# Softmax heads of a hybrid encoder layer: the 640 keys of a query tile split into 384 and 256 columns

## The chip, the cores and the metric

The kernel runs on one core of one Trainium2 chip. The metric is device microseconds of one execution, the median of several. Engines are named as the profile names them: PE is the matrix engine (PEld its weight loads, which run beside the matmuls), DVE the vector engine, ACT the scalar engine with the activation functions, POOL the general engine, SP the engine whose queue issues nearly all DMAs. All data is float32; the matmuls read it as the four-byte type that the profile prints as f32 or fp32r, and precision is kept by splitting a number into a high and a low part.

## The reference

One encoder layer over 2048 positions of width 1024: an attention sub-layer with two groups of eight heads (head width 64), then a squared-ReLU MLP. The change touches the second group, the chunked softmax heads:

```python
CHUNK, LEFT_CHUNKS = 64, 8
BAND = (LEFT_CHUNKS + 1) * CHUNK          # 576
s = jnp.einsum('bnqhd,bnkhd->bnhqk', qc, k_band) * (d ** -0.5)
s = s + bias[None, None]                  # by clipped relative position
s = jnp.where(valid, s, NEG_INF)
p = jax.nn.softmax(s, axis=-1)
out = jnp.einsum('bnhqk,bnkhd->bnqhd', p, v_band)
```

Each chunk of 64 queries sees its own chunk and the eight before it. A tile of 128 queries (two chunks) therefore needs 640 keys, of which a bias of -1e30 masks the 64 that each half does not see.

## The kernel before

**Stages.** Norm and input projections come first, then the attention of both head groups with projections and output-projection rows of other blocks as filler, then the MLP, whose products are formed by a Strassen-like scheme. The sequence is reversed in memory, so "earlier" keys lie at higher columns.

**The attention loop.** Queries are taken in four blocks of 512 (`g`), and the work is a list of units: `SB` (stick-breaking heads) and `CA` (chunked softmax heads). The list is fixed: for the query blocks 2 and 3 together, then 1, then 0, all SB units of the eight heads and then all CA units. Each unit has four steps, one for each tile `qi` of 128 queries. Step *i* of the loop emits, in this order: the transposes (`wt`) of a unit two units back, the softmax or scan of the current tile (`soft1`), the split of the transposed weights into `wth` and `wtl` (`parts`), the exponentials (`soft2`), two value products into `acc`, then the scores of the *next* tile (`scores`), and then as many filler matmuls (`pf`, `po`) as a running credit allows. The credit counts matmuls and steps, not time. PE, DVE, ACT and POOL run in exactly the order in which the program emits; only the DMA issues of this stage on SP may be placed elsewhere by the scheduling layer.

**A CA unit.** There are 32 of them (8 heads, 4 query blocks). For query blocks 0 to 2 all four tiles have 640 keys; in block 3, at the end of the stored sequence, they have 512, 384, 256 and 128. Queries and keys are loaded with a high and a low part: the two parts of a key column lie on partitions 0 to 63 and 64 to 127, and the query tile comes twice, so that two matmuls (`l` = 0 and 1), each with its own weight load from `q`, add up to one score product.

One PSUM bank holds 512 float32 columns, and 640 do not fit in one. So `size` gives `n` = 640 and `hn` = 512: the first 512 columns are the tile `cz`, one bank for each `qi`; the remaining 128 columns of all four tiles are computed at once, when the scores of `qi` = 0 are emitted, into one bank `ct` (four slices of 128 columns).

**What DVE does with it.** `tail(qi)` adds the bias to the `ct` part and takes the running minimum (the kernel works with negated scores), which needs `ct` alone; `soft1(qi)` does the same with the `cz` part and starts from the minimum that `tail` left. In the order of DVE `tail(qi + 1)` stands right behind `soft1(qi)`. Both write one row of scores `s`, which a single ACT instruction of 640 columns turns into exponentials `e`.

**Banks.** `ct`, `cz`, `wt` and the SB scores `z` share four PSUM banks (tag `z`). A new tile takes a bank that has been released, and its first matmul waits for the last reader of the tile before it in that bank.

Of the kernel before, what the change touches and what calls it, by code (L numbers as in the profile page):

```python
# [9 lines left out]
F32 = mybir.dt.float32  # L10
# [8 lines left out]
P = 128  # L19
# [6 lines left out]
TB = 512  # L26
# [53 lines left out]
def encoder_kernel(ctx, tc, xT, c, g1, g2, w_in, w_rest, gqk, bias, w_o, w1, w2, w_ada, b_ada, out):  # L80
# [2 lines left out]
    pe = Ordered(tc, nc.tensor)  # L83
    osp = Ordered(tc, nc.sync)

    WIN = 640
    cpool = ctx.enter_context(tc.tile_pool(name="cpool", bufs=1))
    dram = ctx.enter_context(tc.tile_pool(name="dram", bufs=1, space=DRAM))
    rp = ctx.enter_context(tc.tile_pool(name="rp", bufs=2))
# [5 lines left out]
    pz = ctx.enter_context(tc.tile_pool(name="pz", bufs=4, space=PSUM))  # L95
# [5 lines left out]
    def scratch(name, shape, *counts):  # L101
        return {i: dram.tile(shape, F32, name=name + "_".join(map(str, i))) for i in product(*map(range, counts))}
# [8 lines left out]
    scr_wo = scratch("scr_wo", [P, 2, KT, P], KT)  # L111
    scr_b = scratch("scr_b", [P, WIN], NH)
    scr_h = dram.tile([P, KT, 2, TB], F32, name="scr_h")
# [19 lines left out]
    def column(tag):  # L133
        small[tag].append(small[tag].pop(0))
        return small[tag][-1]
# [103 lines left out]
    if True:  # L239
# [183 lines left out]
        def prepare_bias(h):  # L423
            b = stp.tile([P, WIN], F32, tag="bg", name=f"b{h}", bufs=2)
            sp.dma_start(b, bias[h])

            def rest():
                pool.memset(b[0:HD, WIN - HD :], NEG)
                pool.memset(b[HD:P, 0:HD], NEG)
                sp.dma_start(scr_b[h,], b)  # L430

            behind.add(4, rest)
# [245 lines left out]
    if True:  # L678
# [16 lines left out]
        def load_k(ca, h, tb, n, nm):  # L695
            k = (kp1 if ca else kp0).tile([P, n * TB], F32R, tag=f"k{ca}", name=f"k{ca}_{h}_{nm}")
            r = (h % 2) * HD
            for i in range(n):
                for l in range(2):
                    ldq.dma_start(  # L700
                        k[l * HD : (l + 1) * HD, i * TB : (i + 1) * TB].bitcast(F32),
                        scr_k[ca, tb + i, h // 2][l, r : r + HD],
                    )
            return k
# [42 lines left out]
        class Unit:  # L747


            def __init__(self, h, g, first, last):  # L750
                self.h, self.g, self.first, self.last = h, g, first, last
                self.nm = f"{self.ca}_{h}_{g}"
                self.ws = []
                self.wt = {}
# [30 lines left out]
        class SB(Unit):  # L785
# [27 lines left out]
            def scores(self, qi):  # L813
                nm = f"{self.nm}_{qi}"
                c0 = qi * P if self.diag else 0
                n = TB - c0
                self.z = z = pz.tile([P, TB], F32, tag="z", name=f"z{nm}")
                qs = slice(qi * P, (qi + 1) * P)
                pe.matmul(z[:, :n], self.q[:, 0, qs], self.k[:, c0:], start=True, stop=False)
                pe.matmul(z[:, :n], self.q[:, 1, qs], self.k[:, c0:], start=False, stop=True)  # L820
# [28 lines left out]
        class CA(Unit):  # L849
            ca = 1  # L850

            def __init__(self, h, g):
                super().__init__(h, g, True, True)
                self.weight = 0.9 * (1 if g < NTB - 1 else 0.75)
                self.nk = min(2 * TB, S - g * TB)
                order = [3] + [kb for kb in (4, 2, 1, 0, 5, 6, 7) if kb < self.nk // P]
                self.blocks = [(kb, max(0, kb - 4), min(4, kb + 1)) for kb in order]

            def load(self):
# [6 lines left out]
                self.k = load_k(1, h, g, nk // TB, f"{g}")  # L866
                self.bt = op.tile([P, WIN], F32, tag="bias", name=f"bias{h}_{g}", bufs=2)
                n = min(WIN, nk)
                sp.dma_start(self.bt[:, :n], scr_b[h,][:, :n])
# [7 lines left out]

            def size(self, qi):
                n = min(WIN, self.nk - qi * P)
                return n, min(n, TB)  # L880

            def scores(self, qi):
                nm = f"{self.nm}_{qi}"
                n, hn = self.size(qi)
                if qi == 0 and n > hn:
                    self.tails = pz.tile([P, TB], F32, tag="z", name=f"ct{nm}")
                    for i in range(STEPS):
                        t = self.tails[:, i * P : (i + 1) * P]
                        ks = slice(i * P + TB, i * P + WIN)
                        for l in range(2):  # L890
                            pe.matmul(t, self.q[:, l, i * P : (i + 1) * P], self.k[:, ks], start=l == 0, stop=l == 1)
                self.z = z = pz.tile([P, TB], F32, tag="z", name=f"cz{nm}")
                ks = slice(qi * P, qi * P + hn)
                for l in range(2):
                    pe.matmul(z[:, :hn], self.q[:, l, qi * P : (qi + 1) * P], self.k[:, ks], start=l == 0, stop=l == 1)

            def tail(self, qi):
                nm = f"{self.nm}_{qi}"
                n, hn = self.size(qi)
                s = zp.tile([P, WIN], F32, tag="p", name=f"s{nm}")  # L900
                m = 3e38
                if n > hn:
                    m = column("m0")
                    t = self.tails[:, qi * P : (qi + 1) * P]
                    dve.tensor_tensor_reduce(s[:, hn:n], t, self.bt[:, hn:n], -1.0, 3e38, ALU.add, ALU.min, m)
                self.sm[qi] = (s, m)

# [240 lines left out]
        STEPS = 4  # L1148
# [146 lines left out]
    if True:  # L1295
# [355 lines left out]
        def plain(mb, i):  # L1651

            f = len(steps)
            steps.extend(Second(mb, i, j) for j in range(NP))
            spread = lambda *ns: [f + n for n in ns]
            if i == 6:
                update(mb, 0, 1, spread(0, 1, 2, 8), spread(4, 5, 6, 12))
            if i == 5:
                update(mb, 1, 1, spread(1, 2, 3, 9), spread(6, 7, 8, 13))
                wide = []  # L1660

                def slot(nm):
                    if not wide:
                        t = raw_pair([P, HK, TB], F32, nm)
                        wide.extend(t[:, n, :] for n in range(HK))
                    return wide.pop(0)

                if mb:
                    update(mb, 0, 0, spread(11, 11, 11, 11), spread(16, 16, 17, 17), slot)
                    update(mb, 1, 0, spread(13, 13, 14, 14), spread(18, 18, 19, 19), kept)  # L1670
                else:
                    update(mb, 0, 0, spread(11, 12, 13, 14), spread(16, 17, 18, 19))
                    update(mb, 1, 0, spread(15, 16, 17, 21), spread(20, 21, 22, 25), None, True)
            return f
# [115 lines left out]
        def outer(i, plan):  # L1790

            f = len(steps)
            steps.extend(Outer(i, q, k) for q in range(7) for k in range(HP))
            for g in range(HP // 2):
                for pr, (begin, gap) in plan["load"].items():
                    at(begin + gap * g, lambda pr=pr, g=g: half(i, pr, g))
                for pr, (begin, gap) in plan["sum"].items():
                    at(begin + gap * g, lambda pr=pr, g=g: half_sum(i, pr, g))
            for q in range(7):
                at(f + HP * q - 12, steps[f + HP * q].load)  # L1800
            for pr, b in ((5, "22"), (6, "12"), (2, "11"), (4, "21")):
                s = steps[f + HP * OUTER.index(pr)]
                at(f + HP * OUTER.index(pr) + (1 if b == "22" else -5), lambda s=s, b=b: s.load_x(b))
            return f
# [47 lines left out]
        for mb in (1, 0):  # L1852
# [3 lines left out]
            for j in range(NP):  # L1856
                f = steps[begin + 7 * j]
# [32 lines left out]
        f = plain(0, 1)  # L1890
# [4 lines left out]
        for i, p in ((7, 6), (2, 5), (3, None), (4, None)):  # L1895
            f = outer(i, plan)
# [112 lines left out]
```

## Time and profile before

| | |
|---|---|
| median of 3 runs | 2556.95 us (2555.59 to 2557.69) |
| the profiled execution's own time | 2554.99 us |
| its span, first to last instruction | 2553.3 us |
| PE, share of the span | 99% |
| DVE, share of the span | 79% |
| ACT, share of the span | 59% |
| POOL, share of the span | 29% |
| DMA, mean over the span | 274 GB/s |

The three CA passes lie in the profiled execution at about 571 to 700 us (query blocks 2 and 3, sixteen units), 881 to 960 us (block 1, eight units) and 1204 to 1285 us (block 0, eight units).

How to read the rows: a group row gives line, engine, operation, output and inputs by the program's names, the shape and the count, then the time in which at least one of the group ran, the mean duration of one in ns, and the idle time of the engine before them. Matmuls overlap: one has a duration of 270 to 470 ns from its start to its modelled end, but the next starts much sooner. What a matmul costs PE is therefore the distance from its start to the next start, which the timeline gives: its rows begin with the start in us and the length in us of a run of like instructions. Most helper calls carry line 42, that of the wrapper that keeps the program order.

### The profile page before, as it was taken

The page shows a single profiled execution, that of the slowest core. Times are in us where ns is not written, and L with a number is a line of the kernel's source. Part 1 is how long each engine was busy: PE and PEld are TensorE (multiplying, and loading weights), DVE is VectorE, ACT ScalarE, POOL GpSimd, SP SyncE. Part 2 cuts the span into 40 slices and gives each one's busy share as a digit, 9 for nine tenths or more (in the row PEclk, how much of TensorE's full clock was granted, in tenths as well). Part 3 has the DMA queues.
Part 4 walks back from the last instruction along what each step waited for, and adds up shares of the span by engine and source line. Part 5 has one row for each costly group of instructions (what it writes and reads, how often), then busy time and mean ns, then how long its engine had stood idle before and what let it go on. Part 6 is the DMA issues. An engine that isn't in the chain of part 4 may idle for free. (4 is left out here: it accounts for less than half of the span.)

```text
span 2553.3 us, 39361 instructions
## 1 busy us (share of the span) xinstructions
PE 2528.9 (99%) x12436; PEld 2104.6 (82%) x12436; DVE 2010.0 (79%) x3509; ACT 1496.9 (59%) x2871; POOL 747.7 (29%) x1128
## 2 busy tenths in 40 slices
PE   9999999999999999999999999999999999999999
PEld 7888888888888888887888888888888888888887
DVE  7656767887789878998768777668988766988897
ACT  6333425668866677666755555566555555656565
POOL 4330144776776667776620000000000000000000
PEclk9999999999999999999999999999999999999999
DMA  9879979789977798756787888787899789777772
GB/s 362 324 296 364 343 275 296 214 240 289 277 233 234 242 270 276 254 188 208 213 301 258 301 277 289 252 313 262 277 317 312 262 274 396 273 282 270 286 264 83
DMA packets 293200, 698.92 MB, mean 274 GB/s; under 512 B 31360, under 2 KB 83584, under 8 KB 281856
## 3 DMA queue, kind: packets, MB, share of 16 engines
q1 hardware_dynamic: 291696, 691.69, 79.1%
q10 hardware_dynamic: 1296, 4.72, 0.5%
q8 instruction: 98, 1.61, 0.2%
q14 instruction: 110, 0.90, 0.1%
HBM read 477.66 MB, written 218.63 MB: 273 GB/s over the span
## 5 line engine op out<-in xcount | busy, mean ns | idle before, releaser
L42 PE MATMUL ps<-h,opw 128*128 128x512 f32 x1512 | 358.6, 389 | 0.0
L42 ACT CAST wth<-wt 128x512 fp32r<-128x512 f32 (+3 forms) x544 | 257.4, 484 | 172.5 <-PE wt L42 162.5
L42 POOL TENSOR_TENSOR b<-p 128x512 f32<-128x512 f32 (+1 forms) x320 | 292.5, 914 | 168.0 <-DVE p L42 91.5
L42 DVE TENSOR_TENSOR wtl<-wt,wth 128x512 fp32r<-128x512 f32 (+3 forms) x544 | 290.6, 546 | 59.4 <-ACT wth L42 57.1
L42 PEld LDWEIGHTS ps<-h,opw 128*128 128x128 f32 x1512 | 283.7, 188 | 58.9
L42 PE MATMUL pt<-w,ht 128*128 128x512 f32 x1248 | 288.2, 391 | 0.0
L42 PE MATMUL ps_s<-h,opw 128*128 128x512 f32 x1152 | 277.3, 390 | 0.3 <-ACT cp L42 0.3
L42 PEld LDWEIGHTS pt<-w,ht 128*128 128x128 f32 x1248 | 233.0, 188 | 47.7
L42 DVE TENSOR_TENSOR_SCAN p<-z,p,zero 128x512 f32<-128x512 f32 x192 | 245.6, 1280 | 25.8 <-ACT z L42 18.6
L42 PE MATMUL ps<-oph,opv 128*128 128x512 f32 x1152 | 263.2, 390 | 0.7 <-ACT opv L42 0.6
L42 PEld LDWEIGHTS ps<-oph,opv 128*128 128x128 f32 x1152 | 215.9, 188 | 47.3 <-ACT opv L42 1.5
L42 PEld LDWEIGHTS ps_s<-h,opw 128*128 128x128 f32 x1152 | 215.9, 188 | 46.0 <-ACT cp L42 0.8
L42 PE MATMUL acc<-wth,v 128*128 128x512 f32 (+3 forms) x544 | 220.7, 410 | 0.0
L42 ACT CAST opr<-r 128x512 fp32r<-128x512 f32 x224 | 139.4, 623 | 105.9 <-PE ps L42 50.1
L42 ACT ACTIVATE z<-z 128x512 f32<-128x512 f32 (+1 forms) x320 | 166.5, 521 | 55.3 <-PE z L42 49.5
L42 PE MATMUL z<-k,q 128*128 128x512 f32 (+3 forms) x640 | 185.6, 371 | 7.7 <-DVE p L42 7.0
L42 PE MATMUL acc<-wtl,v 128*128 128x512 f32 (+3 forms) x544 | 185.5, 347 | 0.0
L42 PE MATMUL ps<-opr,ol 128*128 128x512 f32 x768 | 176.4, 389 | 0.1
L42 PE MATMUL wt<-ident,b 128*128 128x128 f32 x1088 | 171.4, 273 | 0.9 <-DVE cols L42 0.3
L42 DVE TENSOR_TENSOR opr<-r,opr 128x512 fp32r<-128x512 f32 x224 | 150.7, 686 | 25.9 <-ACT opr L42 23.3
L42 PEld LDWEIGHTS wt<-ident,b 128*128 128x128 f32 x1088 | 136.4, 141 | 42.1 <-DVE cols L42 1.8
L42 PEld LDWEIGHTS ps<-opr,ol 128*128 128x128 f32 x768 | 144.0, 188 | 30.5 <-DVE ol L42 0.4
(214 smaller groups left out, 4845.6 us busy)
## 6 DMA issues: line engine op xcount, KB each, us to landing
q<-scr_q SPq DMA_DIRECT2D x128, 256.0 KB, 5.0
w<-in_w_dram SPq DMA_DIRECT2D x64, 512.0 KB, 5.7
r<-scr_hid SPq DMA_DIRECT2D x64, 512.0 KB, 7.7
k<-scr_k SPq DMA_DIRECT2D x240, 128.0 KB, 4.5
v<-scr_v SPq DMA_DIRECT2D x120, 256.0 KB, 4.4
wa<-in_w_ada_dram SPq DMA_DIRECT2D x48, 512.0 KB, 6.2
ow<-scr_wo SPq DMA_DIRECT2D x24, 1024.0 KB, 6.5
hw<-scr_hid SPq DMA_DIRECT2D x48, 512.0 KB, 6.6
```

Source lines behind the costliest of these rows:

```text
L42: return lambda *x, **y: self.tc.keep_in_program_order(f(*x, **y))
```

## The change

The bank of the first part is cut at `NEAR` = 384 columns instead of 512, and so the remaining part has 256 columns instead of 128. Four remaining parts of 256 columns need two banks; the first (`qi` 0 and 1) is computed with the scores of `qi` = 0, the second (`qi` 2 and 3) with those of `qi` = 1. The CA units of query block 3 keep their single part.

```diff
-    WIN = 640
+    WIN, NEAR = 640, 384
...
+                self.tails = {}
...
             def size(self, qi):
                 n = min(WIN, self.nk - qi * P)
-                return n, min(n, TB)
+                return n, NEAR if n > TB else n
...
-                if qi == 0 and n > hn:
-                    self.tails = pz.tile([P, TB], F32, tag="z", name=f"ct{nm}")
-                    for i in range(STEPS):
-                        t = self.tails[:, i * P : (i + 1) * P]
-                        ks = slice(i * P + TB, i * P + WIN)
+                if qi < 2 and n > hn:
+                    ct = pz.tile([P, 2, WIN - NEAR], F32, tag="z", name=f"ct{nm}")
+                    for i in (2 * qi, 2 * qi + 1):
+                        self.tails[i] = t = ct[:, i % 2, :]
+                        ks = slice(i * P + NEAR, i * P + WIN)
                         for l in range(2):
                             pe.matmul(t, self.q[:, l, i * P : (i + 1) * P], self.k[:, ks], start=l == 0, stop=l == 1)
...
-                    t = self.tails[:, qi * P : (qi + 1) * P]
+                    t = self.tails.pop(qi)
```

**Where it moves PE's work.** The scores of the first tile of the unit of head 4, query block 0 (names end in the head, the query block and the tile; the last number is a buffer's). Before, behind the value products of the unit before it:

```order
L42 MATMUL acc_1_0_15856<-wth_1_0_0_15878,v_1_0_15557 128x128
L42 MATMUL acc_1_0_15856<-wtl_1_0_0_15879,v_1_0_15557 128x128
L42 MATMUL ct_4_0_0_15925<-k_4_0_15624,q_4_0_15621 128x128 x8
L42 MATMUL cz_4_0_0_15934<-k_4_0_15624,q_4_0_15621 128x512 x2
L42 MATMUL po_1_15702<-fx_5_15299,ow_1_15061 128x512
L42 MATMUL po_1_15702<-fx_6_15301,ow_1_15061 128x512
```

Now:

```order
L42 MATMUL acc_1_0_15876<-wth_1_0_0_15898,v_1_0_15575 128x128
L42 MATMUL acc_1_0_15876<-wtl_1_0_0_15899,v_1_0_15575 128x128
L42 MATMUL ct_4_0_0_15945<-k_4_0_15638,q_4_0_15635 128x256 x4
L42 MATMUL cz_4_0_0_15950<-k_4_0_15638,q_4_0_15635 128x384 x2
L42 MATMUL po_1_15721<-fx_5_15315,ow_1_15077 128x512
L42 MATMUL po_1_15721<-fx_6_15317,ow_1_15077 128x512
```

Four of the eight matmuls of the remaining part are gone from this place, and the others are twice as wide. The other four stand now ahead of the scores of the second tile, as PE's rows one step later show:

```order
L42 MATMUL acc_1_0_15876<-wth_1_0_6_15930,v_1_0_15575 128x256
L42 MATMUL acc_1_0_15876<-wtl_1_0_6_15931,v_1_0_15575 128x256
L42 MATMUL ct_4_0_1_15996<-k_4_0_15638,q_4_0_15635 128x256 x4
L42 MATMUL cz_4_0_1_16001<-k_4_0_15638,q_4_0_15635 128x384 x2
L42 MATMUL po_1_15721<-fx_6_15317,ow_1_15077 128x512 x2
L42 MATMUL po_1_15721<-fx_7_15319,ow_1_15077 128x512
```

Before, the `cz` pair of the second tile followed the `acc` products directly. Everything behind it stands where it stood.

**On DVE** nothing changes its place; the rows of the same unit now (before, the widths were 128, 512 and 128 in the rows of `s`, and the third of these rows read the same `ct` as the first):

```order
L42 TENSOR_TENSOR wtl_1_0_7_15935<-wt_1_0_7_15925,wth_1_0_7_15934 128x128
L42 ISA s_4_0_0_15975,cols<-ct_4_0_0_15945,bias_0_15643 128x256
L42 ISA cols 128x1
L42 ISA s_4_0_0_15975,cols<-cz_4_0_0_15950,bias_0_15643,cols 128x384
L42 ISA cols 128x1
L42 ISA s_4_0_1_15978,cols<-ct_4_0_0_15945,bias_0_15643 128x256
L42 ISA cols 128x1
```

The second `ct` of a unit takes the bank that the first tile's `cz` leaves, and so its first matmul waits for `soft1(0)`, as the second tile's `cz` did before. That `cz` now takes the bank of the first `ct`, and waits for its last reader `tail(1)`, one DVE instruction later. No other wait between the computing engines is new inside a CA unit. On SP the DMAs are the same, but some loads of the attention stage are issued a few places earlier or later.

## The prediction

> **What bounds the kernel now.** I read the page first, then the busy time of each engine in the three CA passes (the view by stretches), because the change acts in these alone.
>
> ```profile
> span 2553.3 us, 39361 instructions
> PE 2528.9 (99%) x12436; PEld 2104.6 (82%) x12436; DVE 2010.0 (79%) x3509; ACT 1496.9 (59%) x2871; POOL 747.7 (29%) x1128
> ...
> core 0: us, PE busy (x) PEld busy (x) DVE busy (x) ACT busy (x) POOL busy (x), PEclk, DMA share, GB/s
> 571.00:700.00 129.00, 125.87 (x767) 107.81 (x767) 95.25 (x356) 106.70 (x266) 91.65 (x91) 1.00 0.94 288
> 881.00:960.00 79.00, 78.43 (x479) 67.09 (x477) 61.98 (x220) 61.67 (x140) 51.26 (x43) 1.00 0.89 275
> 1204.00:1285.00 81.00, 80.03 (x494) 69.09 (x493) 64.52 (x223) 59.86 (x136) 54.03 (x50) 1.00 0.73 214
> ```
>
> PE is the bound: it idles 0.57 us of 79 in the second pass and 0.97 of 81 in the third, and the clock is 1.00 in each. DVE is at 78% and 80% there, ACT at 78% and 74%. The first pass differs: PE idles 3.13 us of 129, ACT is at 83% and the DMA engines at 0.94. So what PE saves in the last two passes should come out at the end almost whole; in the first it may partly turn into waiting.
>
> Busy time does not price a matmul, since matmuls overlap. The price is the distance from start to start, which PE's timeline over one CA unit of the third pass gives:
>
> ```profile
> 1264.70 0.27 PE L42 MATMUL acc<-wtl,v 128*128 128x128 f32 x1
> 1264.81 1.06 PE L42 MATMUL ct<-k,q 128*128 128x128 f32 x8
> 1265.71 0.68 PE L42 MATMUL cz<-k,q 128*128 128x512 f32 x2
> 1266.23 0.85 PE L42 MATMUL po<-fx,ow 128*128 128x512 f32 x3
> ...
> 1268.14 0.28 PE L42 MATMUL acc<-wth,v 128*128 128x256 f32 x1
> 1268.25 0.28 PE L42 MATMUL acc<-wtl,v 128*128 128x256 f32 x1
> 1268.37 0.63 PE L42 MATMUL cz<-k,q 128*128 128x512 f32 x2
> 1268.84 0.62 PE L42 MATMUL po<-fx,ow 128*128 128x512 f32 x2
> ...
> 1272.61 0.34 PE L42 MATMUL acc<-wth,v 128*128 128x384 f32 x1
> 1272.78 0.34 PE L42 MATMUL acc<-wtl,v 128*128 128x384 f32 x1
> 1272.96 0.63 PE L42 MATMUL cz<-k,q 128*128 128x512 f32 x2
> ```
>
> Eight `ct` matmuls of 128 columns take 1265.71 - 1264.81 = 0.90 us, 0.112 each. Two of 512 take 0.47 (1268.37 to 1268.84), 0.235 each. The rows of `acc` give 0.115 for 256 columns and 0.175 for 384. From 256 to 512 the price rises by 0.06 for 128 columns, and on that line 128 columns would cost 0.055. They cost twice that: 128 columns are as dear as 256. And the `cz` pair behind the eight takes 0.52 (1265.71 to 1266.23), 0.05 more than the pair at 1268.37, so the last narrow matmul also delays its successor. I read this as a floor of about 0.11 us below which a matmul with a weight load of its own does not go.
>
> **This is the whole case.** Columns (640) and matmuls (four) per tile stay the same, so under any price that is a straight line in the columns the change saves nothing. It saves only what lies between floor and line.
>
> **The cost on PE.** Only the 24 units with 640 keys change. A second source is each group's busy time divided by its runs of like matmuls, less the mean length, over the others' count:
>
> ```profile
> L42 PE MATMUL cz<-k,q 128*128 128x512 f32 x208 | 67.3, 404 | 0.4 <-DVE cols L42 0.4
> L42 PE MATMUL ct<-k,q 128*128 128x128 f32 x192 | 24.8, 272 | 0.7 <-DVE p L42 0.7
> L42 PE MATMUL cz<-k,q 128*128 128x384 f32 x16 | 4.1, 339 | 0.0
> L42 PE MATMUL cz<-k,q 128*128 128x256 f32 x16 | 3.3, 288 | 0.4 <-DVE cols L42 0.4
> ```
>
> For 256 columns: 3.3 / 8 pairs - 0.288 = 0.124; for 384: 4.1 / 8 - 0.339 = 0.174; for 512: 67.3 / 104 - 0.404 = 0.243; for `ct`: (24.8 / 24 - 0.272) / 7 = 0.109. These hold a few waits and are rounded to 0.1 us, the timeline's to 0.01. I take 0.118 for 256 (between 0.115 and 0.124) and 0.175 for 384. In one unit then:
>
> - `qi` 0: before 0.90 + 0.52 = 1.42. Now 4 x 0.118 + 2 x 0.175 + 0.05 (the first still stands behind a 128-wide `acc`) = 0.87. Saved 0.55.
> - `qi` 1: before 0.47. Now 4 x 0.118 + 2 x 0.175 = 0.82. Added 0.35.
> - `qi` 2 and 3: 0.35 for 0.47 each. Saved 0.24.
>
> The sum is 0.44 saved per unit, 24 x 0.44 = 10.6 us. With 0.124 and 0.174 it is 0.525 - 0.374 + 0.244 = 0.395, or 9.5 us; with the line's floor gone altogether it would be 0. I carry 0.42 as the middle: 10 us.
>
> The Trainium skill ("TensorE: Matmul & The Clock Gate", Back-to-back issue gap) gives about 81 ns for a sustained 128-column matmul and 131 for 512: a straight line through these makes the change worth nothing, and the rows above differ (112 and 235). The same page (LDWEIGHTS) gives 128 weight columns / 1.2 = 107 ns for a load; with the greater of that and N / 2.4 + 2.5 as an estimate, a unit saves 8 x (107 + 216 - 109 - 163) = 408 ns, 9.8 us in all, which this case's rows support.
>
> **The cost on DVE, ACT, POOL and SP.** DVE's instructions keep their count and order; only widths change.
>
> ```profile
> L42 DVE CUSTOM_DVE_ANT_0 s<-cz,bias,cols 128x512 f32<-128x512 f32 x32 | 23.9, 746 | 1.7 <-PE cz L42 1.5
> L42 DVE CUSTOM_DVE_ANT_0 s<-ct,bias 128x128 f32<-128x128 f32 x32 | 9.2, 287 | 3.9 <-PE ct L42 3.2 <-POOL p L42 0.7
> L42 DVE CUSTOM_DVE_ANT_0 s<-cz,bias 128x512 f32<-128x512 f32 x8 | 5.4, 680 | 0.0
> L42 DVE CUSTOM_DVE_ANT_0 s<-cz,bias 128x384 f32<-128x384 f32 x8 | 4.4, 547 | 0.0
> L42 DVE CUSTOM_DVE_ANT_0 s<-cz,bias 128x256 f32<-128x256 f32 x8 | 3.3, 415 | 0.0
> ```
>
> `tail` goes from 287 to 415 ns, `soft1` from 746 to 547 + (746 - 680) = 613: 1028 for 1033 per tile, nothing. ACT, POOL and the DMAs keep theirs. What changes is that PE leaves them 0.42 us less per unit of about 9.8 (the `ct` at 1264.81 and the next unit's at 1274.63), so DVE rises from 80% to about 83%, below PE.
>
> **The new wait.** The second tile's `cz` now waits for `tail(1)` instead of `soft1(0)`, and PE's queue stands behind it: its filler, the transposes of the next step, and through them ACT and DVE. The margin, from the timeline of all engines in the same unit:
>
> ```profile
> 1266.09 0.28 DVE L42 CUSTOM_DVE_ANT_0 s<-ct,bias 128x128 f32<-128x128 f32 x1
> 1266.53 0.75 DVE L42 CUSTOM_DVE_ANT_0 s<-cz,bias,cols 128x512 f32<-128x512 f32 x1
> 1267.20 0.08 DVE L42 DVE_READ_ACCUMULATOR2_ANT cols<- 128x1 f32 x1
> 1267.20 0.29 DVE L42 CUSTOM_DVE_ANT_0 s<-ct,bias 128x128 f32<-128x128 f32 x1
> 1267.41 0.08 DVE L42 DVE_READ_ACCUMULATOR2_ANT cols<- 128x1 f32 x1
> ```
>
> `soft1(0)` is through at 1267.28 and `cz` starts at 1268.37: 1.09 us to spare. Now PE gets there 0.55 sooner, at 1267.82, for the second `ct`; `tail(0)` is 0.13 longer and `soft1(0)` 0.13 shorter, so it is again through at about 1267.3, 0.5 to spare. `tail(1)`, 0.13 longer, ends at about 1267.65 with its read, while PE wants the bank at 1267.82 + 0.47 = 1268.29: 0.6 to spare. I cost it at nothing; DVE's being ahead covers it. If that cover went, every us by which DVE is late would be paid in each of 24 units.
>
> **Where the saving can get stuck.** In the first pass the short units of query block 3 have little filler. Two stalls from its timeline (after the arrow what ended the wait):
>
> ```profile
> 599.33 0.63 PE L42 MATMUL wt<-ident,e 128*128 128x128 f32 x4 [1.03 <-DVE cols L42]
> ...
> 618.09 0.44 PE L42 MATMUL cz<-k,q 128*128 128x128 f32 x2 [1.05 <-DVE cols L42]
> ```
>
> And of the pass's waits (us in total, times, longest) the largest of DVE and of PE:
>
> ```profile
> DVE wtl L42 <- ACT wth L42: 19.3, 37, 1.6
> ...
> PE cz L42 <- DVE cols L42: 1.6, 3, 1.1
> ...
> PE wt L42 <- DVE cols L42: 1.3, 2, 1.0
> ```
>
> PE's end on DVE, which itself waits in this pass for ACT. If PE arrives earlier and the others do not, such a wait grows by what PE saved. Eight of the 24 units lie here (3.4 us of the 10). Bounds: all of it lost, or none; I take 1.2 us lost, nearer to none, since 2.9 us of waits in two kinds are five occurrences for sixteen units. Result: a gain of 8.8 us.
>
> **The rivals.**
>
> 1. *The first pass keeps its length, and the others lose some.* ACT at 83% and DMA at 0.94 speak for it; against it stands that PE is idle there for 2.4% of the time only. Losing all 3.4 us of the first pass and a third of the 6.7 of the others leaves 4.5: 2552.5 us.
> 2. *A straight line prices the matmuls,* as the first of the page's figures would have it, or the floor comes from something else than width. Then the time stays at 2557. The eight `ct` at 0.112 beside 0.115 for 256 columns speak against it.
> 3. *Slower: the second tile's `cz` waits for `tail(1)`.* The two margins of 0.5 and 0.6 us are those of one undisturbed unit; in units where DVE runs later, PE would stop here. It must lose 10 / 24 = 0.42 us per unit to eat the gain, that is DVE must be a whole us later than in the rows above, in all units. At 0.7 per unit the result is 24 x 0.7 - 10 = 6.8 us slower, 2564. DVE at 80% speaks against it.
> 4. *That the change doesn't do what it says* (fewer narrow matmuls) is excluded by the order shown above.
>
> **How the numbers follow.** The sum stands against the profiled execution: 2554.99 - 8.8 = 2546.2. The median of the runs, 2556.95, lies 1.96 above that execution, so for the median I say 2548.1. A measurement of this kernel can tell about 0.2% (5.1 us) from no change. Forecast, a gain of 5.1 to 11.4 us: 0.84. Rival 1: 0.07, of which 0.01 would still count as faster. Rival 2: 0.03. Rival 3: 0.06. So faster 0.85, same 0.09, slower 0.06. The range reaches from a gain of 11.4 (11.0, the highest sum of the rows with 0.115, plus the runs' spread) to one of 4.0: 2545.5 to 2553.0, which leaves out about 0.13 above and 0.04 below.
>
> **What would show it.** `ct` must appear as 192 matmuls of 128x256 with about 0.118 from start to start, `cz` with 208 of 128x384 and 16 of 128x512. From the first `ct` to the filler behind it, a unit's 1.42 us must become about 0.87. The second and third pass must be about 3.4 us shorter each, the first by 2 or more, and the rest of the span unchanged. DVE's group for `ct` must read about 415 ns, for `cz` about 613. Wrong I would be if PE's waits for DVE before `ct` and `cz` (under 2 us now) grew to several us, if the passes kept their length while PE's idle time rose, or if 256-wide `ct` matmuls stood 0.15 us or more apart, since eight of them a unit then cost 0.26 more and most of the gain is gone.

## The result and the profile after

| | before | after |
|---|---|---|
| median of 11 runs each | 2557.03 us (2555.59 to 2558.37) | 2550.11 us (2548.36 to 2553.2) |
| ratio, 95% interval | | 0.9973 [0.9964, 0.9983] |
| the profiled execution's own time | 2554.99 us | 2549.72 us |
| its span | 2553.3 us | 2548.0 us |

The change gains 6.9 us; the interval reaches from 4.3 to 9.2. The forecast was a gain of 8.8 and a time of 2548.1. One execution of the kernel before, of 6549.87 us, is left out of all comparisons below.

The page of the changed kernel, span and busy time of the engines:

```profile
span 2548.0 us, 39355 instructions
PE 2520.9 (99%) x12436; PEld 2104.0 (83%) x12436; DVE 2010.0 (79%) x3509; ACT 1498.6 (59%) x2871; POOL 747.0 (29%) x1128
```

PE has 12436 matmuls as before and is busy 8.0 us less; DVE's busy time is the same to the tenth of a microsecond. The groups that changed, on PE and on DVE (busy us, mean ns of one, idle time before them):

```profile
L42 PE MATMUL cz<-k,q 128*128 128x384 f32 x208 | 54.3, 342 | 0.5 <-DVE cols L42 0.4
L42 PE MATMUL ct<-k,q 128*128 128x256 f32 x192 | 31.6, 287 | 1.7 <-DVE cols L42 1.0 <-DVE p L42 0.7
L42 DVE CUSTOM_DVE_ANT_0 s<-cz,bias,cols 128x384 f32<-128x384 f32 x96 | 58.7, 611 | 3.9 <-PE wt L42 0.5
L42 DVE CUSTOM_DVE_ANT_0 s<-ct,bias 128x256 f32<-128x256 f32 x96 | 40.3, 419 | 1.5 <-PE ct L42 1.2 <-issue 0.3
```

The counts are the 192 and 208 that the order showed. `tail` takes 419 ns and `soft1` 611, forecast 415 and 613. New is 1.0 us of waiting for `cols`, a result of DVE, ahead of `ct`: before, `ct` waited for DVE's `p` alone (0.7 us), which it still does.

**The price of the matmuls.** PE's timeline over one unit of the third pass: the second `ct`, then the `cz` of tiles 1, 2 and 3, then the next unit's first `ct` and `cz` (start, length, count of the run):

```profile
1261.89 0.64 PE L42 MATMUL ct<-k,q 128*128 128x256 f32 x4
1262.37 0.52 PE L42 MATMUL cz<-k,q 128*128 128x384 f32 x2
1262.72 0.62 PE L42 MATMUL po<-fx,ow 128*128 128x512 f32 x2
...
1264.41 0.52 PE L42 MATMUL cz<-k,q 128*128 128x384 f32 x2
1264.77 0.86 PE L42 MATMUL po<-fx,ow 128*128 128x512 f32 x3
...
1266.72 0.52 PE L42 MATMUL cz<-k,q 128*128 128x384 f32 x2
1267.08 0.62 PE L42 MATMUL po<-fx,ow 128*128 128x512 f32 x2
...
1268.28 0.69 PE L42 MATMUL ct<-k,q 128*128 128x256 f32 x4
1268.81 0.51 PE L42 MATMUL cz<-k,q 128*128 128x384 f32 x2
1269.15 0.40 PE L42 MATMUL po<-fx,ow 128*128 128x512 f32 x1
1269.83 1.06 PE L42 MATMUL wt<-ident,e 128*128 128x128 f32 x8 [0.28 <-DVE wtl L42]
```

From start to start the first tile takes 1269.15 - 1268.28 = 0.87 us, the second 1262.72 - 1261.89 = 0.83, the third and fourth 0.36 each: 2.42 us a unit. Before it was 1.42 + 3 x 0.47 = 2.83. So 0.41 is saved per unit, 9.8 us in 24 units. (The last row, a wait, comes up again below.)

**Where it comes out.** The three passes in stretches that begin at a pass's first `ct` and end at the same matmul in both kernels, 25 matmuls behind the pass's last `cz`. Columns: stretch, its length, busy time of PE, PEld, DVE, ACT, POOL with their instructions, granted clock, DMA share, GB/s. Before:

```profile
571.30:702.40 131.10, 127.97 (x782) 109.84 (x781) 95.64 (x356) 108.84 (x269) 92.32 (x92) 1.00 0.92 283
881.80:962.20 80.40, 79.83 (x488) 68.40 (x487) 62.04 (x221) 63.32 (x144) 52.73 (x44) 1.00 0.90 279
1205.00:1286.70 81.70, 81.45 (x505) 70.74 (x506) 64.36 (x226) 60.56 (x139) 55.19 (x49) 1.00 0.72 210
```

After:

```profile
571.50:699.50 128.00, 124.96 (x783) 109.65 (x781) 95.32 (x356) 108.78 (x269) 92.21 (x92) 1.00 0.94 290
878.90:957.70 78.80, 77.54 (x489) 68.43 (x489) 61.53 (x221) 63.26 (x144) 52.48 (x44) 1.00 0.87 258
1200.70:1280.40 79.70, 78.75 (x505) 70.72 (x505) 63.88 (x225) 60.50 (x139) 54.91 (x49) 1.00 0.73 215
```

With 0.41 a unit, each pass should be 3.3 us shorter. By the starts in the traces (to 0.01 us) the first is shorter by 3.17, the second by 1.65, the third by 1.98: 6.80 in all. In the first pass PE's idle time stays (131.10 - 127.97 = 3.13, then 3.04); in the second it grows from 0.57 to 1.26 and in the third from 0.25 to 0.95. So 3.0 of the 9.8 us are lost, nearly all in the second and third pass.

**The longest wait** is one in the second pass. PE's timeline of that unit before (after the arrow what ended a wait):

```profile
900.12 1.00 PE L42 MATMUL ct<-k,q 128*128 128x128 f32 x8
900.96 0.68 PE L42 MATMUL cz<-k,q 128*128 128x512 f32 x2
901.48 1.03 PE L42 MATMUL wt<-ident,e 128*128 128x128 f32 x8
...
903.05 0.40 PE L42 MATMUL acc<-wtl,v 128*128 128x512 f32 x1
903.68 0.50 PE L42 MATMUL cz<-k,q 128*128 128x512 f32 x1 [0.23 <-DVE cols L42]
```

The same unit after, all engines:

```profile
896.71 0.65 PE L42 MATMUL ct<-k,q 128*128 128x256 f32 x4
...
897.19 0.51 PE L42 MATMUL cz<-k,q 128*128 128x384 f32 x2
...
898.42 0.69 DVE L42 TENSOR_TENSOR stf<-pf,stf 128x512 fp32r<-128x512 f32 x1 [0.60 <-ACT stf L42]
...
899.03 0.41 DVE L42 CUSTOM_DVE_ANT_0 s<-ct,bias 128x256 f32<-128x256 f32 x1
899.12 0.40 PE L42 MATMUL acc<-wtl,v 128*128 128x512 f32 x1
...
899.59 0.62 DVE L42 CUSTOM_DVE_ANT_0 s<-cz,bias,cols 128x384 f32<-128x384 f32 x1
900.13 0.08 DVE L42 DVE_READ_ACCUMULATOR2_ANT cols<- 128x1 f32 x1
...
900.27 0.74 PE L42 MATMUL ct<-k,q 128*128 128x256 f32 x4 [0.76 <-DVE cols L42]
```

From the unit's first `ct` to the second tile's first score matmul it is 903.68 - 900.12 = 3.56 us before and 900.27 - 896.71 = 3.56 after. Between them runs a chain over DVE: it waits for ACT's half of a filler product's split (`stf`), does its own half in 0.69 us, and only then the softmax of the first tile, which releases the bank. PE's own work in between shrank by 0.5 us, the chain did not, so PE waits longer by what it saved: the `ct` comes 900.27 - 899.12 = 1.15 us behind the last `acc`, where 0.23 is normal behind 512 columns (899.12 - 898.88 for the `acc` before it was 0.24), so 0.92 are lost here. Before it was 903.68 - 903.05 = 0.63 behind the last `acc`, that is 0.40 lost: the wait grew by 0.52, nearly all that the first tile had saved. At the entry of the third pass the same is seen; before:

```profile
1204.99 1.11 PE L42 MATMUL ct<-k,q 128*128 128x128 f32 x8 [0.73 <-DVE p L42]
1205.94 0.68 PE L42 MATMUL cz<-k,q 128*128 128x512 f32 x2
1206.76 0.44 PE L42 MATMUL wt<-ident,b 128*128 128x128 f32 x2
```

After:

```profile
1200.70 0.74 PE L42 MATMUL ct<-k,q 128*128 128x256 f32 x4 [0.72 <-DVE p L42]
1201.28 0.62 PE L42 MATMUL cz<-k,q 128*128 128x384 f32 x2
1202.47 0.55 PE L42 MATMUL wt<-ident,b 128*128 128x128 f32 x3 [0.57 <-DVE p L42]
```

From `ct` to `wt` it is 1.77 us in both: the scan `p` of the SB unit ahead sets that moment, and the `ct` and `cz` done faster only end in a longer wait for it. The third pass loses nearly as much again in its last unit, where a transpose waits for DVE's `wtl` (the last row of the unit shown above): it starts 1269.83 - 1269.15 = 0.68 us behind the filler, where it was 1276.27 - 1276.04 = 0.23 in the kernel before, so 0.45 are lost.

The rest of the attention stage keeps its length but for small differences (the stretches between the passes 179.40 and 179.45, 242.78 and 243.02 us; from the third pass to the first `pso`, which ends the stage, 34.55 and 35.07). That `pso` starts at 1321.22 before and at 1315.47 after; the part behind it takes 1232.06 and 1232.53. These differences outside the passes add up to some 1.5 us, and so the two profiled executions differ by 5.3 us and not by 6.8; the change's second profile (below) shows that they scatter.

### The profile page after: what moved, and what is told of

Read it like the earlier page. It is cut to its first block, busy times and chain, and to the rows that moved or that the text cites. A ratio compares the mean times of both kernels' runs of the same rounds, so it can differ in the third digit from the quotient of the medians.

```text
span 2548.0 us, 39355 instructions
## 1 busy us (share of the span) xinstructions
PE 2520.9 (99%) x12436; PEld 2104.0 (83%) x12436; DVE 2010.0 (79%) x3509; ACT 1498.6 (59%) x2871; POOL 747.0 (29%) x1128
## 4 chain that ended last, share of the span: by engine, by line
PE 83%; DVE 6%; DMA 3%; ACT 3%; issue 2%; POOL 1%; SPq 0%; DVEq 0%; ACTq 0%; POOLq 0%
PE ps L42 27%; PE ps_s L42 14%; PE pt L42 11%; PE acc L42 6%; PE wt L42 6%; PE pf L42 4%; PE z L42 4%; PE po L42 4%; PE pq L42 3%; DVE p L42 2%; PE cz L42 2%; DMA hw<-in_w_dram 1%; PE ct L42 1%; DVE opr L42 1%; ACT z L42 1%
```

## The experiments

The theory F is that of the prediction: a floor of about 0.11 us per matmul with its own weight load, and so a saving only where narrow matmuls are replaced. N is a rival by which matmuls under 256 columns run at a lower rate rather than at a floor, P that the new place of the matmuls, not their width, brings the gain. Theory W, formed from the traces, says that what is missing to the sum went into the waits for DVE shown above.

### The cut at 448 columns: floor or rate

```diff
-    WIN, NEAR = 640, 384
+    WIN, NEAR = 640, 448
```

> The cut at 448 + 192 columns, everything else as in the change (two tiles of two remaining parts). Theory F (a floor: a matmul with its own weight load takes about 0.112 us however narrow, and from 256 columns up the price is a line through 0.118 and 0.235): 192 columns cost the floor, 0.112, and 448 cost 0.205, so PE saves 8 x 0.03 = 0.24 us per unit, 5.8 in all, of which some 2.5 to 3 are lost in waits as in the change: about 2554, between the two kernels, `ct` 0.112 apart. Rival N (narrow matmuls, under 256 columns, run at half rate: 0.112 is 128 columns at twice the price): 192 columns cost 0.168 to 0.177, PE loses 8 x 0.03 per unit instead: about 2563, slower than before, `ct` 0.17 apart. A straight line: 2557.

2552.63 us, ratio 0.9985 [0.9976, 0.9994]: 5.2 us faster than before. PE's timeline of a unit's second tile:

```profile
1263.25 0.59 PE L42 MATMUL ct<-k,q 128*128 128x192 f32 x4
1263.67 0.59 PE L42 MATMUL cz<-k,q 128*128 128x448 f32 x2
1264.10 0.62 PE L42 MATMUL po<-fx,ow 128*128 128x512 f32 x2
```

Four of 192 columns take 0.42 us, 0.105 each in this unit (the median distance over the whole trace is 0.112), no more than 128 columns did (0.112); two of 448 take 0.43. 192 columns still lie on the floor, and the gain is that of the narrower `cz` pairs. N falls, and so does the straight line of rival 2: 448 + 192 are the same 640 columns.

The kernel before has still narrower matmuls, eight of a single column at the start of the program:

```profile
12.49 1.05 PE L42 MATMUL pva<-ones,nsaa 128*128 128x1 f32 x8 [0.63 <-DVE nsaa L42]
13.40 2.25 PE L42 MATMUL idle<-ones 128*128 128x128 f32 x18
```

One column costs (13.40 - 12.49) / 8 = 0.114 us, as much as 128: the floor does not depend on the columns. What sets it stays open. Every matmul here has a weight load of its own (PE and PEld both count 12436), so no run separates the load from another fixed cost of a matmul.

### Two tiles for the remaining part, cut as before: structure alone

```diff
-    WIN, NEAR = 640, 384
+    WIN, NEAR = 640, 512
```

> The structure of the change alone: the cut stays at 512 + 128, but the four remaining parts stand in two tiles of two, computed with the scores of the first and second query tile. Theory F (the gain comes from the widths, and the two tiles bring only waits): PE's work is that of before plus 0.05 us per unit (a second run of narrow matmuls delays its successor), and PE reaches the second tile 0.45 us sooner, where it waits for DVE: 2558 to 2560, slower than before by 1 to 3 us. Rival P (the gain comes from where the second half of the remaining parts was put, not from the widths): 2550, as the change.

2556.35 us, ratio 0.9998 [0.9989, 1.0007]: no difference. Four of the eight 128-column matmuls stand here ahead of the second tile's scores, as in the change, and no gain shows: P falls. The slowdown that I had expected of F here did not come either; the new order of bank releases costs nothing measurable while PE's work keeps its length.

### The disputed price, doubled

The remaining part's products are formed twice; in the kernel before,

```diff
-                        for l in range(2):
+                        for l in (0, 1, 0, 1):
```

and the same edit in the changed kernel. Each adds 192 matmuls, here of 128 and there of 256 columns.

> The kernel before, with the eight matmuls of the remaining parts (128 columns) issued twice into the same bank. F and N: 8 x 24 more at 0.112 us each, 21.5 us, less up to 1 us of waits that they cover: 2577 to 2579. A straight line through the prices of 256 and 512 columns (0.055 for 128): 10.6 us, 2568.

> The change, with the matmuls of the remaining parts (256 columns) issued twice into the same bank. Theory F: 8 x 24 more at 0.118 us, 22.7, less 1 to 2.7 us of waits that they cover: 2570 to 2573, so as much over the change as the doubled 128-column matmuls cost over before (20.3), for twice the columns. A straight line in the columns: twice that, 2590.

The 128-column kernel takes 2576.95 us, ratio to before 1.008 [1.0064, 1.0096], 19.1 more than the 2557.83 of its session. The 256-column one takes 2569.49, ratio 1.0046 [1.0032, 1.006], 19.4 more than the change's 2550.11. With four runs each these are good to about 4 us; in the traces the three passes are longer by 19.8 and by 19.0 us. Twice the columns, the same addition. PE's timeline with 16 of 128 columns:

```profile
1262.44 1.95 PE L42 MATMUL ct<-k,q 128*128 128x128 f32 x16
1264.22 0.68 PE L42 MATMUL cz<-k,q 128*128 128x512 f32 x2
```

And with 8 of 256:

```profile
1269.47 1.12 PE L42 MATMUL ct<-k,q 128*128 128x256 f32 x8
1270.43 0.52 PE L42 MATMUL cz<-k,q 128*128 128x384 f32 x2
```

These are 1.78 / 16 = 0.111 and 0.96 / 8 = 0.120 us each, so 192 more would be 21.4 and 23.0 us. What came out is less, by about 2.3 and 3.6 us (1.6 and 4.0 by the passes). Added work is partly taken up by waits that PE had anyway: its idle time in the three passes falls from 3.95 to 3.45 us and from 5.25 to 3.59. That is W's effect with the sign reversed, and it covers a part of the difference.

### Filler ahead of the second tile's scores

```diff
+                if u.ca and st == 1:
+                    fill(front.weight, turns.get(i, 0))
                 u.scores(st)
...
-            fill(front.weight if front else 0.6, turns.get(i, 0))
+            if i + 1 >= len(steps) or not (u.ca and st == 1):
+                fill(front.weight if front else 0.6, turns.get(i, 0))
```

> The change, with the filler of the step put ahead of the second tile's scores instead of behind them (24 + 8 steps). Theory W (the missing 2 to 3 us of the gain went where PE arrives at the second tile's bank before DVE has released it, because it saved 0.55 us just ahead): PE has 0.5 to 0.9 us of other work there, the waits of PE before `ct` (1.0 us in the second pass) go, 2547.5 to 2549. Rival D (the missing part is spread noise, DMA order or the first pass): 2550, no change. If DVE then starves for the later scores: 2552.

2549.49 us, ratio 0.9969 [0.996, 0.9978]; by the time it can't be told from the change. In its trace the shorter of the two waits ahead of `ct` (929.36 in the change) is gone, the longer one is there as before (0.92 us beyond the normal distance): in that step the credit gives no filler, so there was nothing to put ahead.

### The two DVE jobs one step later

DVE's half of a filler split (`stf`) and one sum (`xr`) were held back by a step where they stood ahead of the first tile's softmax (`stored` holds the jobs that the filler has handed over).

```diff
+                    stored.add(got)
...
+            hold = fs == STEPS - 1 and i + 1 < len(steps) and steps[i + 1][0].ca and steps[i + 1][0].g < NTB - 1
...
-                job()
+                if hold and job in stored:
+                    soon.append(job)
+                else:
+                    job()
```

> The change, with two DVE jobs moved: where the filler's own evacuation (the split of `stf`, the sum `xr`) would fall due just ahead of a unit's first `tail` and `soft1`, it goes one step later. That moves one `stf` and one `xr` instruction, both in the second pass. Theory W (PE's new waits before the second `ct` are DVE being late by its own other work, which a PE that arrives 0.55 us sooner now meets): the two long stalls before `ct` in the second pass (0.93 and 0.37 us beyond the normal distance) go, 1.0 to 1.3 us, PE reaches the end of the attention at about 1314.3 instead of 1315.5; 2549. Rival B (the wait is the new order of banks itself): they stay, 2550.

Both waits go. PE's timeline of the unit shown above, now:

```profile
896.24 0.65 PE L42 MATMUL ct<-k,q 128*128 128x256 f32 x4
...
898.65 0.40 PE L42 MATMUL acc<-wtl,v 128*128 128x512 f32 x1
...
898.88 0.63 PE L42 MATMUL ct<-k,q 128*128 128x256 f32 x4
```

The second `ct` follows after 2.64 us in place of 3.56, without a wait; some of it comes back as 0.25 and 0.41 us some matmuls later. The second pass, as one stretch:

```profile
878.50:956.40 77.90, 77.35 (x488) 68.33 (x487) 61.18 (x221) 62.98 (x144) 52.32 (x44) 1.00 0.87 260
```

77.9 us against 78.8 in the change and 80.4 before, with PE idle for 0.55 as before (0.57). So in this pass the `stf` and `xr` jobs were the cause of about half of the loss (0.8 of 1.6 us): W holds there. The attention stage ended at 1312.92 us, where 1314.3 was expected; the stretches outside the passes, which scatter by more than 1 us, are part of that. The median of the runs, 2550.72 (ratio 0.9974 [0.9962, 0.9985]), does not show it; 0.9 us is below what the runs can tell.

### The extra filler at a pass's start one step earlier

```diff
-        turns = {STEPS * n: 4 if u.ca else 8 for n, u in enumerate(units) if n and u.ca != units[n - 1].ca}
+        turns = {STEPS * n - u.ca: 4 if u.ca else 8 for n, u in enumerate(units) if n and u.ca != units[n - 1].ca}
```

> The change, with the four extra filler matmuls at the start of a pass of CA units given one step earlier, ahead of the first unit's first step. Theory W: at the start of the second and third pass PE finds work while DVE ends the scans, and the stalls there (0.74 and 0.26 us in the third, 0.32 and 0.20 in the second) shrink: 0.5 to 1.2 us less, 2549 to 2549.6. If DVE's lag only moves to the next wait: no change.

Not as expected: 2551.73 us, ratio 0.9978 [0.997, 0.9987]. The wait at the entry of the third pass stays (0.57 us of idle time ahead of 1204.84, as in the change ahead of 1202.47), and a step further on, where the filler now lacks, a new one appears:

```profile
910.91 1.07 PE L42 MATMUL wt<-ident,e 128*128 128x128 f32 x8 [0.97 <-DVE wtl L42]
```

The second pass is 79.2 us long, 0.5 more than in the change, and the first 131.0, 3.0 more, of which 1.7 are a lowered clock (last section); most of the rest is a new wait for DVE near that pass's start (0.64 us idle at 578.55), behind the filler that was moved ahead. So DVE's lag only moved to the next wait, as the second forecast said, and that cost time. For the third pass the cause of the loss at its entry is therefore named (the scan `p`), but no edit here removed it.

### All three together

> The change with all three: filler ahead of the second tile's scores, the two DVE jobs later, the start of a pass given its filler one step earlier. Theory W: the gains add up, 2 to 3 us under the change: 2547 to 2548, the attention through at about 1312.5 to 1313.5. Rival B or D: 2549 to 2550.

2551.97 us, ratio 0.9978 [0.9969, 0.9988], again not as expected: the gains do not add up. The second pass takes 79.15 us with the new wait of the edit before, where the held jobs alone gave 77.94. The first takes 129.27, 1.3 more than in the change, with the clock at 1.00 throughout, and the attention stage ends at 1315.84.

### The change again, and the two useful edits together

> The changed kernel once more, unaltered, beside the next one on the same chip. Expected: 2549 to 2551 us, ratio about 0.9973, attention part ending within 1 us of 1315.5 us if the places of PE's waits are set by the order of the program; if the waits move from execution to execution, the long wait of 0.8 to 0.9 us at about 900.3 us should be found elsewhere or not at all.

> The change with filler ahead of the second tile's scores and with the two DVE jobs held back by a step. Theory W (the waits for DVE ahead of the second tile's scores took what was missing to the sum): both edits remove such waits, so the attention part should end at about 1312 to 1313 us, 2.5 to 3.5 earlier than in the change, and the runs should give about 2547 us, ratio 0.996. Rival M (what is missing lies in the noise of the MLP part): no difference to the change in the same call, 2549 to 2551.

The change again gives 2550.05 us, ratio 0.9973 [0.9963, 0.9984]; its passes take 127.83, 78.70 and 79.73 us (127.97, 78.73 and 79.70 in the first profile), and the long wait is the same: the second `ct` starts 899.40 - 895.84 = 3.56 us behind the first, with 0.76 us of idle time. So these waits are set by the order of the program, not by chance. The attention stage ended at 1313.84, 1.6 us earlier than in the first profile, where within 1 was expected: the stretches outside the passes scatter by that much.

The two edits together give 2550.22 us, ratio 0.9972 [0.9962, 0.9983], no difference to the change. Their second pass is 77.88 us as W expects, their first 129.28, 1.3 more than the change's; in that one profile the clock was lowered there (see the last section). The attention stage ended at 1315.44, not at 1312 to 1313. The expected 2547 was not seen, and M can't be excluded by the medians.

The medians hide some of it, because the granted clock of an execution is 1.000, 0.999 or 0.998 (once 0.997). Among the runs at 1.000 alone the medians are:

| kernel | runs at 1.000 | median us |
|---|---|---|
| before (three sessions) | 21 | 2556.3 |
| the change (both sets of runs) | 10 | 2549.3 |
| filler first | 5 | 2548.7 |
| held jobs | 2 | 2548.4 |
| both edits | 3 | 2548.5 |
| all three | 5 | 2550.4 |
| earlier filler | 1 | 2550.4 |

The change gains 7.0 us by this comparison. The filler ahead of the scores and the held jobs may be worth 0.6 to 1 us more, in the direction that W says, but with two to five runs each this is not shown; the earlier filler goes the other way.

## Why the prediction was right, point by point

**The floor and the price of 10 us: right.** Forecast was 0.42 per unit; the rows give 0.41, 9.8 us in 24 units, with 0.87 for the first tile (forecast 0.87), 0.83 for the second (0.82) and 0.36 for the others (0.35). The doubled matmuls, the cut at 448 and the matmuls of one column show the floor; whether the weight load sets it, as the prediction's wording suggests, is not shown. Rival 2, the straight line, is refuted. The Trainium skill's sustained figures ("TensorE: Matmul & The Clock Gate", Back-to-back issue gap: about 81 ns at 128 columns, 131 at 512) do not hold for these four-byte matmuls, which stood 111 and 235 ns apart; its figure for a weight load (LDWEIGHTS, 128 / 1.2 = 107 ns) lies within 5% of the floor measured here.

**DVE neutral: right.** 419 and 611 ns for 415 and 613 forecast, and the same sum of busy time. Its share in the third pass went from 79% to 80% (63.88 of 79.70 us), not up by three points as forecast, since the pass became 2.0 us shorter and not 3.4.

**The new wait costed at nothing: the mis-sized term.** "DVE's being ahead covers it" was read from one unit in which DVE had no filler job ahead of the softmax. The cover held in most units, but in the one at 896.71 DVE came 0.92 us late, in another at 929.36 by 0.37, both ahead of the second `ct`, which waits for `soft1(0)` and for which the margin worked out was 0.5; the `cz` behind `tail(1)`, with its 0.6, was not held up there. Before the change the first of these two places had 0.40 us of the 0.92 already, the second none. Rival 3 had the right engine and said where it would hurt ("in units where DVE runs later"), but its title names the wrong bank release, and it came true in two units of the eight in that pass and not in all. With these, the entry and the last unit of the third pass and some smaller waits, the second pass lost 1.6 us and the third 1.3 of their 3.3, where I had costed nothing. So the sign "about 3.4 us shorter each" was not met in these two passes (1.65 and 1.98).

**The 1.2 us stuck in the first pass: wrong.** That pass gave 3.17 of 3.3. The two waits I feared for are there as before: 599.33 and 618.09, now 598.63 and 617.11, each 1.2 us beyond the normal distance in both kernels. They lie in units of query block 3, which the change leaves alone. My reading is that such a wait grows only if the shortened work lies between the start of the chain and the place where PE waits for it; in block 3's units nothing was shortened, so PE and chain came earlier together. That agrees with both kinds of places, but no run here was made to test it.

So the sum was 10 - 1.2 = 8.8, and what came is 9.8 - 3.0 = 6.8 in the passes. The medians' 6.9 agree. That the forecast came this close is partly luck: the 1.2 us were charged to the first pass, where nothing was lost, and stood in for a part of the 3.0 lost mostly in the others. Rival 1 (the first pass keeps its length) had the place of the loss reversed.

## What to carry to other kernels

Price a short matmul by the distance from start to start at each width in the trace: where the price stops falling with the width, columns can be moved from wide matmuls to narrow ones for nothing until these leave the floor. Before counting a saving on the engine that sets the end, look for the waits behind it whose chain over other engines begins ahead of the shortened work: such a wait grows by the whole saving, so the saving counts once per unit that has no such wait. Read the margin of a wait in the unit where the waiting-for engine has extra jobs, not in a quiet one.

## What the runs showed of the hardware

The granted clock can fall to half for some microseconds right after PE has waited, and whether it does differs between executions. The wait of 1.05 us in the first pass (query block 3, a `cz` of 128 columns) is in all twelve profiles at the same place; behind it the clock fell in two of them (the earlier filler, and both edits). Stretches before, behind and after that wait in the kernel with the earlier filler:

```profile
613.00:619.00 6.00, 4.65 (x32) 3.71 (x30) 4.22 (x15) 5.09 (x14) 4.90 (x5) 1.00 0.85 271
619.00:623.00 4.00, 3.92 (x18) 3.66 (x18) 2.96 (x16) 3.23 (x11) 2.28 (x4) 0.57 1.01 301
623.00:629.00 6.00, 6.00 (x39) 5.34 (x38) 4.21 (x15) 3.40 (x9) 2.82 (x3) 1.00 1.00 336
```

The same three stretches in the change have 1.00 throughout; here the middle one has 0.57, and PE got through 18 matmuls in it where the change got through 27:

```profile
617.00:621.00 4.00, 3.80 (x27) 3.54 (x28) 3.42 (x19) 3.75 (x11) 2.67 (x4) 1.00 0.96 300
```

4 us at 0.57 are 1.7 us of PE's time; inside, from 619.45 to 622.85, the clock is 0.50. In the kernel with filler first a wait of 1.76 us in the MLP part was followed by 5 us at 0.66, again 1.7 us. A clock of 0.998 or 0.999 for a whole execution can thus be a few such dips: the profile at 0.998 (both edits) holds the one behind the wait and another at its start, 6.8 us at 0.50 from 14.8 us. The kernel before shows the same spread of clocks. What decides on a dip was not tried. So a wait can cost more than its own length, and a gain of 1 us can't be read from medians here without looking at the clock.

Matmuls of 192 columns cost no more than those of 128 (0.105 and 0.111 us), and matmuls of a single column no less (0.114 us).
